# Feed-forward by seven products of halves, in a layer on one core

## The chip, the core and the metric

The program runs on one of the eight cores of a Trainium2 chip. A core has TensorE (PE in the profile, with its weight loads as PEld), VectorE (DVE), ScalarE (ACT), GpSimd (POOL) and SyncE (SP), which here issues the transfers. Operands lie in SBUF, 128 partitions wide; TensorE writes to PSUM, eight banks of 512 float32 columns for each partition. The metric is the device time of the whole program in microseconds, as the median of several runs.

## The reference

One layer of a decoder with two streams: a prompt of 1024 tokens and a sample of 64, side by side as N = 1088 tokens. After two kinds of attention and an attention over a memory comes the feed-forward, to which the change belongs. The model is 1024 wide, the features within are 2816. All is float32.

```python
def mem_attend(h, mk, mv, w_mq, g_mq, w_mo):
    b, t, _ = h.shape
    q = rms_norm((h @ w_mq).reshape(b, t, H_M, HEAD_DIM_M), g_mq)
    return attend(q, mk, mv, None, None).reshape(b, t, D_MODEL) @ w_mo

def conv_ffn(h, prev, w_up, w_conv, b_conv, w_down):
    gu = h @ w_up
    gate, val = gu[..., :D_FF], gu[..., D_FF:]
    t = gate.shape[1]
    gp = jnp.concatenate([prev.astype(gate.dtype), gate], axis=1)
    conv = sum(gp[:, j:j + t] * w_conv[j] for j in range(CONV_W)) + b_conv
    y = (jax.nn.silu(conv) * val) @ w_down
    return y, gp[:, -(CONV_W - 1):]
...
        xp = xp + mem_attend(rms_norm(xp, g_norm2[l]), mk, mv, w_mq[l], g_mq[l], w_mo[l])
        f, conv_p = conv_ffn(rms_norm(xp, g_norm3[l]), zeros_prev, w_up[l], w_conv[l], b_conv[l], w_down[l])
        xp = xp + f
```

## The kernel before

**Precision.** Every matrix product is done as three. Each operand is split into a high part in a reduced float32 form (fp32r) and a low part, the rest. ACT casts the high part, and POOL or DVE subtracts it for the low one. `SPLIT` (three pairs) then multiplies high by high, high by low and low by high into the same PSUM bank.

**Order.** The program is written as one list of instructions, from which the build makes a queue for each engine, and the semaphores between them. Within a queue, instructions run in the order that the build fixed. `place` puts extra steps behind certain pieces of a product. SyncE's queue holds the transfers.

**Activations** lie transposed: eight blocks of 128 rows of the model's width, with the 1088 tokens along the columns. `CHUNKS` cuts these into 384, 384 and 320. A `Product` (872) is one block of 128 outputs for one chunk: `gemm` (859) goes through eight blocks of rows with three matmuls each, 24 in all.

**Weights** come through `Stream` (831). It fetches halves of a block of columns (128 x 512, 256 KB, line 840), three on their way, and splits four ahead: ACT casts (848), POOL subtracts (849). The list `srcs` holds the order: `w_o`, `w_mq`, `w_mo`, then `w_up`.

**Memory output projection.** `project` (984) takes `oT`, the memory attention's output in two parts, through `w_mo` in 8 x 3 products; beside the first of them lies the rest of the attention. For each product DVE adds the residual (1001), SyncE stores the sum to DRAM (1002), ACT and DVE make the two parts of the next operand times the norm's gain (1004, 1005), ACT squares and POOL sums the squares (1011). `after_mo` (1191) makes the root mean squares of a chunk with a matmul of ones (1194), whose result multiplies the up projection's outputs, later.

**Feed-forward.** 22 tiles of 128 features run one after the other (`Tile`, 1235). `run` goes through the gate's three chunks: DVE multiplies each by the norm into a padded row (1269). Then comes the convolution: an ACT pass (1272), two DVE passes over 1090 columns (1274), Silu on ACT (1276), the norm again on POOL (1280). The value's three chunks follow: DVE multiplies (1287), ACT and POOL split the result (1288, 1289). Between their pieces lies the down projection of the tile before (`down`, 1292): for 8 blocks of outputs and 3 chunks three matmuls each (1298), whose results DVE adds to `y` in SBUF (1305). `split_down` splits the tile's down weights on ACT and POOL (1255, 1256).

Of the kernel before, what the change touches and what calls it, by code (L numbers as in the profile page):

```python
# [33 lines left out]
CHUNKS = ((0, 384), (384, 384), (768, 320))  # L34


@with_exitstack
def hybrid_step(ctx: ExitStack, tc: tile.TileContext, i: dict, o: dict):
# [3 lines left out]
    def f32(ap):  # L42
        return ap.bitcast(F32)
# [48 lines left out]
    ps = ctx.enter_context(tc.tile_pool(name="ps", bufs=1, space=PSUM))  # L92
# [58 lines left out]
    def load_x(c, z):  # L151
        """Half of the columns of 256 tokens, or of the sample's 64."""
# [45 lines left out]
    # K, V and Q of a pair of heads over 256 tokens  # L198
# [14 lines left out]
    def qk_norm(p, sq, raw, eps_ap, rows):  # L213
        """q and k of raw [rows, 256], each head's normed, twice in a row; k with its gain, for the cache."""
# [16 lines left out]
    def gained(hi, lo, src, g, rows=slice(0, P)):  # L231
        """The two parts of src with the gain of its rows; the second of some rows alone."""
# [17 lines left out]
    def place(main, subs):  # L250
        """main, and after some of its parts others."""
# [6 lines left out]
    def proj(p, t, subs):  # L258
        """One block of tokens through a pair's columns, woven with subs; what is to be done with it later."""
# [79 lines left out]
    def forget():  # L339
        """log sigmoid of the forget logits, and their running sums."""  # L340
# [4 lines left out]
        # z = exp(-|f|); log1p(z) = log(u) - ((u - 1) - z) / u with u = 1 + z  # L345
# [44 lines left out]
    def toeplitz(head, q, n):  # L390
        """Row r of q reads the head's reversed table from 128 - r on."""
# [20 lines left out]
    class Attn:  # L412
        """Two blocks of 128 queries of one head."""
# [106 lines left out]
    def substeps(slow=False):  # L520
        """What runs between a projection's products: scores of the next head, values of the one before."""
# [54 lines left out]
    # ------------------------------------------------------------------ memory keys and values, sample's attention  # L576
# [70 lines left out]
    class Sample:  # L647
        """The sample's 64 queries of both heads of a pair, one above the other."""
# [94 lines left out]
        def turn(self, c):  # L743
            """Weights of four blocks of 128 keys, or of the new ones, turned."""
# [79 lines left out]
    late_left = ExitStack()  # L824
    stream = None

    # ------------------------------------------------------------------ products with streamed weights
    srcs = [i[n][m][:, 4 * c:4 * c + 4] for n, nm in (("w_o", 8), ("w_mq", 8), ("w_mo", 8)) for m in range(nm) for c in range(2)]
    srcs += [i["w_up"][m][:, 4 * c:4 * c + 4] for f in range(NF) for m in (f, NF + f) for c in range(2)]

    class Stream:
        """Halves of 128 columns of weights in the order of their use, four of them split, three on their way."""
# [10 lines left out]
        def upto(self, n):  # L843
            while self.n < min(n, len(srcs)):
# [4 lines left out]
                pool.tensor_tensor(lo, raw, f32(hi), op=ALU.subtract)  # L849
# [4 lines left out]
        def done(self, j):  # L854
            """Half j isn't used any more."""
# [3 lines left out]
    def gemm(out, j, x, c, end):  # L859
        """The products of halves j and j + 1 with a chunk of tokens, in eight pieces."""  # L860
        c0, cn = CHUNKS[c]

# [9 lines left out]
    class Product:  # L872
        """A chunk of 128 outputs' products, its tile taken at the first."""

        def __init__(self, j, x, c, end, tag="pj"):
            self.tag, self.t = tag, None
            self.pieces = gemm(self.out, j, x, c, end)
# [9 lines left out]
    def parts(pl, name):  # L887
        """Two parts of eight rows of all tokens."""
        return [[pl.tile([P, N + 4], F32R, name=f"{name}{x}{k}")[:, :N] for k in range(KT)] for x in range(2)]

    def open_left():
        nonlocal stream
        left.close()
        ha = late_left.enter_context(tc.tile_pool(name="ha", bufs=1, side="left"))
        stream = Stream(late_left.enter_context(tc.tile_pool(name="wr", bufs=1, side="left")))
        x = late_left.enter_context(tc.tile_pool(name="x0", bufs=1, side="left")).tile([P, 384], F32, name="x0")
        nc.sync.dma_start(x, i["xT"][0, :, 0:384])
        stage = rest.enter_context(tc.tile_pool(name="stage", bufs=1, side="left"))
# [57 lines left out]
    # ------------------------------------------------------------------ output projection  # L956
# [7 lines left out]
    def wide():  # L964
        return [[t[:, k] for k in range(KT)] for t in (hb.tile([P, KT, N], F32R, name=x) for x in ("hhi", "hlo"))]

    BUFS = {"qhi": 2, "qlo": 2, "kvraw": 2, "s": 3}

    def tmp(tag, shape):
        return pl.tile(shape, F32R, name=tag, bufs=BUFS.get(tag, 1))  # L970

    def row(tag, n=384):
        """A row of float32 in a slot of this tag."""
        shape = [P, 2, 384] if tag in ("qhi", "qlo") else [P, 2, 256]
# [9 lines left out]
    def project(j, x, order, firsts, res, out, nxt, gi, accs, after):  # L984
        """res + x @ w, to DRAM; its two parts times the next norm's gain; its squares' sums."""
# [33 lines left out]
    h2 = wide()  # L1019
# [13 lines left out]
    # ------------------------------------------------------------------ memory attention  # L1033
# [3 lines left out]
    oT = parts(ha, "a")  # L1037
# [18 lines left out]
    class Mem:  # L1056
        """A head's attention of a chunk of tokens."""
# [7 lines left out]
        def query(self):  # L1065
            """The products, and what follows each half of them."""
# [72 lines left out]
        def value(self, d):  # L1139
# [28 lines left out]
    for n, u in enumerate(mems):  # L1168
# [4 lines left out]
        def move(h, what):  # L1173
            """Splits this and loads the one after the next."""
# [13 lines left out]
    h3 = wide()  # L1188
    norms = {}

    def after_mo(c, acc):
        cn = CHUNKS[c][1]
        st = bank("PT")[:, :cn]
        pe.matmul(st, ones, acc[:, :cn], start=True, stop=True)  # L1194
        ms, y, a = row("qlo", 768), row("qlo", 768), None
        ms, y, a = ms[:, 0:cn], ms[:, 384:384 + cn], y[:, 0:cn]
        dve.tensor_scalar(ms, st, EPS, None, op0=ALU.add)
        act.activation(y, ms, ACT.Ln)
        act.activation(y, y, ACT.Exp, scale=-0.5)
        dve.tensor_tensor(a, ms, y, op=ALU.mult)  # L1200
# [221 lines left out]
```

## Time and profile before

| | us |
|---|---|
| median of 3 runs | 1882.5 |
| runs | 1881.01 to 1883.11 |
| span of the profiled execution | 1878.9 |
| its end of TensorE's work | 1874.8 |

The span goes from the first to the last instruction of one profiled execution; the runs' time is that of the whole program. The page's second part shows the span in 40 slices, busy tenths of each engine, and the clock that TensorE was granted:

```profile
PE   6899999999997899999999999999999999999999
DVE  6777766767766875334443345445545545555546
ACT  5656666767766665335543332212212212222220
POOL 5646666877976443434433444434434434443441
PEclk9999999999998999999999999999999999999999
```

A slice is 47 us, and the feed-forward takes the last 17 of them. The parts shown below use the same columns as the page: a group's line, engine, operation, output and inputs, shapes and count, then its busy time and the mean of one in ns, then the idle time of its engine before it and what ended that. In the timeline the first number is the start, the second the length.

### The profile page before, as it was taken

The page shows a single profiled execution, that of the slowest core. Times are in us where ns is not written, and L with a number is a line of the kernel's source. Part 1 is how long each engine was busy: PE and PEld are TensorE (multiplying, and loading weights), DVE is VectorE, ACT ScalarE, POOL GpSimd, SP SyncE. Part 2 cuts the span into 40 slices and gives each one's busy share as a digit, 9 for nine tenths or more (in the row PEclk, how much of TensorE's full clock was granted, in tenths as well). Part 3 has the DMA queues.
Part 4 walks back from the last instruction along what each step waited for, and adds up shares of the span by engine and source line. Part 5 has one row for each costly group of instructions (what it writes and reads, how often), then busy time and mean ns, then how long its engine had stood idle before and what let it go on. Part 6 is the DMA issues. An engine that isn't in the chain of part 4 may idle for free.

```text
span 1878.9 us, 31543 instructions
## 1 busy us (share of the span) xinstructions
PE 1808.8 (96%) x11426; PEld 1754.7 (93%) x11426; DVE 1071.5 (57%) x2537; ACT 800.9 (43%) x1828; POOL 937.4 (50%) x1312
## 2 busy tenths in 40 slices
PE   6899999999997899999999999999999999999999
PEld 5789999999996788999999999999999999999999
DVE  6777766767766875334443345445545545555546
ACT  5656666767766665335543332212212212222220
POOL 5646666877976443434433444434434434443441
PEclk9999999999998999999999999999999999999999
DMA  8312122212216776421113433111111111111102
GB/s 276 89 45 68 43 76 77 63 55 76 60 34 177 248 227 196 144 67 52 60 52 122 137 104 106 45 40 51 40 45 51 35 51 45 40 51 40 45 23 97
DMA packets 111339, 157.49 MB, mean 84 GB/s; under 512 B 15480, under 2 KB 75000, under 8 KB 111184
## 3 DMA queue, kind: packets, MB, share of 16 engines
q1 hardware_dynamic: 111184, 155.48, 26.6%
q8 instruction: 90, 1.47, 0.3%
q14 instruction: 65, 0.53, 0.1%
HBM read 125.40 MB, written 33.18 MB: 84 GB/s over the span
## 4 chain that ended last, share of the span: by engine, by line
PE 54%; POOL 1%; issue 1%; ACT 0%; DVE 0%; POOLq 0%; DVEq 0%; ACTq 0%
PE pj L866 37%; PE PT L1298 7%; PE tq L1298 3%; PE O L1298 3%; PE S L1110 1%; PE O L1146 1%; PE tq L1146 1%; POOL lo L849 1%; PE PT L1133 0%; PE O L1110 0%; PE PT L1091 0%; POOL s L1125 0%; PE PT L1194 0%; ACT hi L848 0%; PE PT L1026 0%
## 5 line engine op out<-in xcount | busy, mean ns | idle before, releaser
L866 PE MATMUL pj<-hhi,hi 128*128 128x384 f32 (+1 forms) x1248 | 412.8, 331 | 0.0
L866 PE MATMUL pj<-hlo,hi 128*128 128x384 f32 (+1 forms) x1248 | 408.8, 328 | 0.0
L866 PE MATMUL pj<-hhi,lo 128*128 128x384 f32 (+1 forms) x1248 | 408.3, 327 | 0.0
L849 POOL TENSOR_TENSOR lo<-raw,hi 128x512 fp32r<-128x512 f32 x136 | 176.9, 1302 | 336.7 <-ACT hi L848 336.0
L848 ACT CAST hi<-raw 128x512 fp32r<-128x512 f32 x136 | 84.1, 620 | 406.5 <-issue 253.0
L866 PEld LDWEIGHTS pj<-hhi,hi 128*128 128x128 f32 x1248 | 234.5, 188 | 0.5
L866 PEld LDWEIGHTS pj<-hlo,hi 128*128 128x128 f32 x1248 | 234.6, 188 | 0.1
L866 PEld LDWEIGHTS pj<-hhi,lo 128*128 128x128 f32 x1248 | 234.4, 188 | 0.1
L1305 DVE TENSOR_TENSOR a<-PT,a 128x384 f32<-128x384 f32 (+1 forms) x252 | 133.9, 531 | 158.2 <-PE PT L1298 158.2
L268 PE MATMUL pj<-whi,xhi 128*128 128x384 f32 (+1 forms) x512 | 195.5, 382 | 7.9 <-ACT xhi L126 6.7
L866 PE MATMUL pj<-a,hi 128*128 128x384 f32 (+1 forms) x736 | 183.5, 331 | 3.6 <-DVE qhi L1001 1.7
L268 PE MATMUL pj<-whi,xlo 128*128 128x384 f32 (+1 forms) x512 | 175.7, 343 | 5.9 <-DVE xlo L127 5.9
L268 PE MATMUL pj<-wlo,xhi 128*128 128x384 f32 (+1 forms) x512 | 177.2, 346 | 2.9 <-POOL wlo L119 2.9
L866 PEld LDWEIGHTS pj<-a,hi 128*128 128x128 f32 x736 | 129.4, 188 | 6.2 <-DVE a L909 2.5
L454 ACT ACTIVATE s<-s,mx 128x640 f32<-128x640 f32 (+7 forms) x128 | 94.2, 736 | 79.1 <-DVE mx L452 77.5
L491 DVE TENSOR_TENSOR ptl<-PT,pth 128x512 fp32r<-128x512 f32 (+2 forms) x192 | 99.6, 522 | 38.8 <-ACT pth L490 36.5
L866 PE MATMUL pj<-a,lo 128*128 128x384 f32 (+1 forms) x368 | 120.7, 329 | 0.0
L220 POOL TENSOR_TENSOR r<-m,mhalf 128x4 f32<-128x4 f32 (+1 forms) x72 | 73.8, 1025 | 90.0 <-DVE m L219 80.0
L268 PEld LDWEIGHTS pj<-whi,xhi 128*128 128x128 f32 x512 | 100.0, 196 | 8.9 <-ACT xhi L126 6.7
L268 PEld LDWEIGHTS pj<-whi,xlo 128*128 128x128 f32 x512 | 98.0, 191 | 6.6 <-DVE xlo L127 6.6
L268 PEld LDWEIGHTS pj<-wlo,xhi 128*128 128x128 f32 x512 | 99.6, 195 | 4.5 <-POOL wlo L119 4.5
L490 ACT CAST pth<-PT 128x512 fp32r<-128x512 f32 (+2 forms) x192 | 85.1, 449 | 38.2 <-PE PT L489 36.8
(443 smaller groups left out, 4465.2 us busy)
## 6 DMA issues: line engine op xcount, KB each, us to landing
raw<-in_w_up_dram SPq DMA_DIRECT2D x88, 256.0 KB, 2.6
kvraw<-in_w_down_dram SPq DMA_DIRECT2D x44, 256.0 KB, 2.5
wraw<-in_w_dram SPq DMA_DIRECT2D x56, 192.0 KB, 2.4
mwraw<-in_w_mkv_dram SPq DMA_DIRECT2D x16, 512.0 KB, 5.6
s<-in_xn_dram SPq DMA_DIRECT2D x8, 512.0 KB, 6.8
mixd<-mix SPq DMA_DIRECT2D x32, 128.0 KB, 1.8
bias<-negc SPq DMA_DIRECT2D x8, 512.0 KB, 3.6
raw<-in_w_o_dram SPq DMA_DIRECT2D x16, 256.0 KB, 3.5
```

What stands on the lines that cost most here:

```text
L220: pool.tensor_tensor(r[:rows], m[:rows], mhalf[:rows, 0:4], op=ALU.pow)
L268: pe.matmul(pj[:, :nw], x2[a][:, k, t * P:(t + 1) * P], wt[k][b][:, :nw], start=n == 0, stop=n == 3 * KT - 1)
L454: act.activation(s[:, :n], s[:, :n], ACT.Exp, bias=mx, scale=-1.0, accum_out=sm)
L490: act.copy(hi[:, f:f + n, j], pt[:, f:f + n])
L491: dve.tensor_tensor(lo[:, f:f + n, j], pt[:, f:f + n], f32(hi[:, f:f + n, j]), op=ALU.subtract)
L848: act.copy(hi, raw)
L849: pool.tensor_tensor(lo, raw, f32(hi), op=ALU.subtract)
L866: pe.matmul(out()[:, :cn], w[a][:, k % 4], x[b][k][:, c0:c0 + cn], start=k == 0 and n == 0, stop=k == KT - 1 and n == 2)
L1110: pe.matmul(sp[:rows], self.q[a][:, d, t * P:t * P + rows], k[b][:, d], start=n == 0, stop=n == 5)
L1146: pe.matmul(op[:, a0:a1], v[x][:, b, d * P:(d + 1) * P], self.p2[y][:, b, a0:a1], start=n == 0, stop=n == 5)
L1298: pe.matmul(d[:, :cn], self.wd[x][m // 4][:, (m % 4) * P:(m % 4 + 1) * P], self.a[w][:, c0:c0 + cn], start=z == 0, stop=z == 2)
L1305: dve.tensor_tensor(dst, d[:, :cn], dst, op=ALU.add)
```

## The change

Two matrices cut in halves both ways can be multiplied with seven products of halves in place of eight, if sums of the halves are formed before and after. The change does this with the feed-forward's two projections. For each, A is the weights and B the activations; H = 544 is half of the tokens and Q = 272 half of that.

- **The products.** M1 = A11 B11, M2 = A12 B21, M5, M6, M7, M3 and M4 use sums. Up, an output tile is two blocks of 128 features that are 11 blocks apart (`n` even: two gate blocks, odd: the two value blocks of the same features). Each product is 4 blocks of rows x 3 split pairs x 2 quarters of 272 columns, 24 matmuls.
- **Sums of results in PSUM.** M6, M7 and M4 go on top of M1 in one tile of two banks (chain X), M3 on top of M5 (Z), M2 alone (T). ACT copies M1, M5 and M6 out to SBUF before the next one lands on top; DVE reads the four results.
- **Sums of weights** and all splits of the feed-forward are made by DVE, with ACT's cast; `prepare` runs five products ahead, with seven places for split operands and seven for raw quarters.
- **Sums of activations** (right sums) for the up projection are made during the memory output projection, which now runs for the first half of the tokens and then, with `w_mo` fetched and split again, for the second half. The low parts of the second round's weights are DVE's.
- **Between the projections** the products of gate and value go to DRAM (`ad`), and come back as B's quarters.
- **Down**, one product runs through all 11 steps of features for four output blocks at a time, in four PSUM tiles, before the next product begins; the last two steps run together, block by block. The order is M2, M1, M5, M3, M6, M7, M4. `prepare_down` runs two steps ahead, with three places for the right operand and five for the left. The residual's rows are loaded into `y` before; at the end of M1 ACT copies its result out, and over the steps that follow POOL adds the copy to two other quarters and the residual to a third.

The core of the diff:

```diff
-srcs = [i[n][m][:, 4 * c:4 * c + 4] for n, nm in (("w_o", 8), ("w_mq", 8), ("w_mo", 8)) for m in range(nm) for c in range(2)]
-srcs += [i["w_up"][m][:, 4 * c:4 * c + 4] for f in range(NF) for m in (f, NF + f) for c in range(2)]
+srcs = [i[n][m][:, 4 * c:4 * c + 4] for n, ms in (("w_o", range(8)), ("w_mq", range(8)), ("w_mo", ROWS), ("w_mo", ROWS)) for m in ms for c in range(2)]
...
-                pool.tensor_tensor(lo, raw, f32(hi), op=ALU.subtract)
+                (dve if self.n >= 48 else pool).tensor_tensor(lo, raw, f32(hi), op=ALU.subtract)
...
+CHAIN = {"M1": "X", "M6": "X", "M7": "X", "M4": "X", "M2": "T", "M5": "Z", "M3": "Z"}
+order = [(n, x) for n in range(NF) for x in ("M1", "M2", "M6", "M5", "M7", "M3", "M4")]
...
+def prepare(g):
...
+    if what == "M6":
+        dve.tensor_tensor(a21, a21, a22, op=ALU.add)
+        dve.tensor_tensor(a11, a21, a11, op=ALU.subtract)
+    if what == "M7":
+        dve.tensor_tensor(a21, a22, a11, op=ALU.subtract)
+    if what == "M3":
+        dve.tensor_tensor(a12, a12, a11, op=ALU.subtract)
+    two_parts(hi, lo, src)
...
+def t_sums(m, x):
+    j = m % 4
+    if m < 4:
+        dve.scalar_tensor_tensor(t, x, g3[m], told[j], op0=ALU.mult, op1=ALU.subtract)
+        two_parts(*quarter_of("12", j), t)
+    else:
+        t = t12[j]
+        dve.scalar_tensor_tensor(t, x, g3[m], t, op0=ALU.mult, op1=ALU.subtract)
+        two_parts(*tsum["M6"][j], t)
+        gained_parts(m, *quarter_of("22", j), x)
+        dve.tensor_tensor(told[j], t, told[j], op=ALU.subtract)
+        dve.tensor_tensor(told[4 + j], told[4 + j], t, op=ALU.subtract)
...
+def finish(n, what, w):
+    if what in ("M1", "M5", "M6"):
+        kept[n, what] = temps.take()
+        act.copy(halves(kept[n, what]), both(w))
+        return
+    r, z, other = {"M2": (0, 0, "M1"), "M7": (1, 1, "M5"), "M3": (0, 1, "M6"), "M4": (1, 0, None)}[what]
+    if is_gate:
+        gate.into(r, z, w, t)
+    elif t is None:
+        value(gate, r, z, w, None)
+    else:
+        add(t, w, t)
+        value(gate, r, z, None, t)
...
+for g, (n, what) in enumerate(order):
+    w = product(n, what, lambda p, j: hi_lo[p][:, j * P:(j + 1) * P], 4, [right(what, j) for j in range(4)], True, True)
+    if g == 0:
+        t3_parts()
+        norm3(1)
+        t4_parts()
+    finish(n, what, w)
+    while prepared < min(len(order), g + 1 + AHEAD):
+        prepare(prepared)
+        prepared += 1
...
+def prepare_down(s):
...
+    if what == "M5":
+        dve.tensor_tensor(S, S, a["A22"], op=ALU.add)
+        dve.tensor_tensor(b12, b12, b11, op=ALU.subtract)
+    if what == "M3":
+        dve.tensor_tensor(S, S, a["A11"], op=ALU.subtract)
+        dve.tensor_tensor(a["A12"], a["A12"], S, op=ALU.subtract)
...
+    two_parts(*la, left)
+    two_parts(*ra, right)
...
+for s, (what, f) in enumerate(steps):
+    if f < NG - 1:
+        prepare_down(s + 2)
+        load_a()
...
+            load_b(DOWN[nxt], f)
...
+    for m in range(4):
+        for x in ((s,) if f < NG - 2 else (s, s + 1)):
+            la, ra = down_ops[x]
+            for z in range(2):
+                for y, (p, b) in enumerate(SPLIT):
+                    pe.matmul(ws[m][:, z, :Q], la[p][:, m * P:(m + 1) * P], ra[b][:, z * Q:z * Q + Q],
+                              start=first and y == 0 and what in opening, stop=final and y == 2 and what in closing, skip_group_check=True)
+        if f == NG - 2:
+            finish_down(what, m, ws[m])
```

`Gate.into` adds a result and the kept copy into the padded row on DVE (in three pieces for the second half of the tokens), and starts `conv` for a block once both halves are in: DVE multiplies by the norm, ACT's pass, two DVE passes of 1090, Silu on ACT, and DVE multiplies by the norm again. `two_parts` is ACT's cast and DVE's subtraction. `value` multiplies with the gate on DVE and stores to `ad`. `finish_down` adds a block's result in PSUM to its rows of `y` on DVE.

More of the change, by code (lines that the diff above doesn't have):

```diff
@@ L1018, in hybrid_step @@
     dve.memset(e2, 1.0)
-    h2 = wide()
+    h2 = [[t[:, k] for k in range(KT)] for t in (hq.tile([P, KT, N], F32R, name=x) for x in ("hhi", "hlo"))]
     def after_o(c, acc):
@@ L1186, in hybrid_step @@
         place(u.query(), subs)
[L1188 to L1198, printed above, removed]
+    queries.close()
+    hr = ctx.enter_context(tc.tile_pool(name="hr", bufs=1, side="right", reuse_waits="tile"))
@@ new lines, in hybrid_step, with wide_rows, halves, both @@
+    PLACES = ("11", "21", "12", "22")
+    def wide_rows(b, p, dt=F32R):
+        return hr.tile([P, 4, H], dt, name=f"h{b}{p}")
+    h3 = {b: [wide_rows(b, p) for p in range(2)] for b in PLACES[:2]}
+    accs, rs = [None, None], [None, None]
+    g3 = [gcol[:, 2, m:m + 1] for m in range(KT)]
+    def halves(ap):
+        return ap.rearrange("p (z q) -> p z q", z=2)
+    def both(w):
+        return w[:, :, :Q]
+    def like(ap, src):
+        return ap if len(src.shape) == 2 else halves(ap)
+    def long_row(tag):
+        return row(tag, 768)[:, :H]
@@ L1199, in after_mo, with norm3 @@
+    def norm3(z):
+        w = wides.take()
+        for q in range(2):
+            pe.matmul(w[:, q, :Q], ones, accs[z][:, q * Q:q * Q + Q], start=True, stop=True)
+        a, y = (long_row("qlo") for _ in range(2))
+        rs[z] = long_row(("ptl", "sq")[z])
+        dve.tensor_scalar(halves(a), both(w), EPS, None, op0=ALU.add)
+        act.activation(y, a, ACT.Ln)
         act.activation(y, y, ACT.Exp, scale=-0.5)
-        dve.tensor_tensor(a, ms, y, op=ALU.mult)
+        dve.tensor_tensor(a, a, y, op=ALU.mult)
@@ L1212, in hybrid_step @@
-    for n, g in enumerate(project(32, oT, ORDER, [], x1d, xd, h3, 2, ("kPh", "kPl", "kSh"), after_mo)):
-        subs = [(at - 8 * n, f) for at, f in last if 0 <= at - 8 * n < 8] + take()
-        if n == 2:
-            subs += [(0, lambda: mems[-1].value(0)), (1, lambda: mems[-1].value(1))]
-        place(g.pieces, subs)
-    rows_ = [ha.tile([P, N + 4], F32R, name=f"a{x}{k}") for x in range(2) for k in range(KT)]
-    y = [f32(r) for r in rows_[:8]]
-    acts = [[rows_[8 + 2 * b + z][:, :N] for z in range(2)] for b in range(2)]
@@ new lines, in hybrid_step, with right, product @@
+    tsum = {}
+    def right(what, j):
+        if what in ("M1", "M2", "M3", "M5"):
+            return quarter_of({"M1": "11", "M2": "21", "M5": "12", "M3": "22"}[what], j)
+        return tsum[what][j]
+    chains = {}
+    def product(key, what, a, k, rights, begin, end):
+        chain = key, CHAIN[what]
+        if chain not in chains:
+            chains[chain] = wides.take()
+        w = chains[chain]
+        fresh, final = what in ("M1", "M2", "M5"), what in ("M4", "M2", "M3")
+        for z in range(2):
+            for j in range(k):
+                for x, (p, b) in enumerate(SPLIT):
+                    pe.matmul(w[:, z, :Q], a(p, j), rights[j][b][:, z * Q:z * Q + Q],
+                              start=fresh and begin and j == 0 and x == 0, stop=final and end and j == k - 1 and x == 2, skip_group_check=True)
+        return w
@@ new lines, in hybrid_step @@
+    for w_, m in enumerate(ROWS):
+        nc.sync.dma_start(told[m], xd[m, :, 0:H])
+        act.mul(told[m], told[m], g3[m])
+    for n, m in enumerate(ROWS):
+        x = long_row("qhi")
+        nc.sync.dma_start(x, x1d[m, :, H:N])
+        w = wides.take()
+        for q in range(2):
+            place(gemm(lambda: w[:, q], 48 + 2 * n, oT[1], (q * Q, Q), q == 1), [])
+            if n == 0 and q == 0:
+                norm3(0)
+        evict_mo(m, 1, 0, H, both(w), x)
+        wides.give(w)
+        t_sums(m, x)
@@ new lines, in hybrid_step @@
+    sums = [row("qlo", 768)[:, :512], row("qlo", 768)[:, :512]] + [row(x, 768)[:, :512] for x in ("pth", "ptl", "sq")]
+    sums += [f32(flat(x)) for x in ("vSh", "vSl", "vPh", "vPl", "kSh", "kSl")]
+    raws = Slots([lambda: f32(flat("kvraw"))] * 2 + [lambda: stream_place("raw")] * 3)
+    parts_ = Slots([lambda: (stream_place("hi"), stream_place("lo"))] * 4 + [lambda: (flat("kPh"), flat("kPl"))])
+    NEEDS = {"M2": ("A12",), "M1": ("A11",), "M5": ("A21", "A22"), "M3": ("A11", "A12"), "M6": (), "M7": ("A22",), "M4": ("A22",)}
@@ new lines, in hybrid_step, with load_a @@
+    loads = [(s, a) for s, (what, f) in enumerate(steps) for a in NEEDS[what]]
+    downs = {}
+    def load_a():
+        while loads:
+            s, a = loads[0]
+            f = steps[s][1]
+            if a == "A21":
+                t = sums[f]
+            elif raws.free:
+                t = raws.take()
+            else:
+                break
+            loads.pop(0)
+            downs[s, a] = t
+            r, c = int(a[1]) - 1, int(a[2]) - 1
+            nc.sync.dma_start(t, i["w_down"][f + c * NG, :, r * 512:r * 512 + 512])
```

371 lines of the change are left out of this document (276 added, 95 removed).

## The prediction

> **What bounds the kernel now.** I read the page first, then the busy time by stretch, cut where the lines change.
>
> ```profile
> span 1878.9 us, 31543 instructions
> PE 1808.8 (96%) x11426; PEld 1754.7 (93%) x11426; DVE 1071.5 (57%) x2537; ACT 800.9 (43%) x1828; POOL 937.4 (50%) x1312
> 0.00:977.60 977.60, 914.15 (x6026) 862.76 (x6027) 619.19 (x1707) 595.57 (x1502) 576.00 (x900) 0.98 0.34 104
> 977.60:1082.30 104.70, 104.49 (x643) 103.46 (x642) 38.75 (x73) 39.58 (x82) 43.49 (x43) 1.00 0.40 124
> 1094.30:1876.00 781.70, 780.47 (x4711) 779.91 (x4709) 408.12 (x749) 159.95 (x235) 309.58 (x362) 1.00 0.17 52
> ```
>
> The stretches are PE, PEld, DVE, ACT, POOL, then granted clock, DMA share, GB/s. Up to 977.6 the code stays; from there to 1082.3 runs the memory output projection, then the feed-forward. There TensorE is busy 780.47 of 781.70 us at clock 1.00, VectorE about half. Only TensorE's work counts, so the first question is what one matmul costs at the new width of 272 columns (before: 384, 384, 320). A matmul's recorded length overlaps its neighbours; the pitch of starts is the cost.
>
> ```profile
> 1400.14 0.34 PE L866 MATMUL pj<-hhi,hi 128*128 128x384 f32 x1
> 1402.05 0.34 PE L866 MATMUL pj<-hhi,lo 128*128 128x384 f32 x1
> 1409.42 0.31 PE L866 MATMUL pj<-hhi,hi 128*128 128x320 f32 x1
> 1411.03 0.31 PE L866 MATMUL pj<-hhi,lo 128*128 128x320 f32 x1
> 911.78 0.28 PE L1110 MATMUL S<-kPh,qhi 128*128 128x256 f32 x1
> 912.38 0.28 PE L1110 MATMUL S<-kPh,qlo 128*128 128x256 f32 x1
> 908.83 0.28 PE L1146 MATMUL O<-pth,vSl 128*128 128x64 f32 x1
> 909.16 0.28 PE L1146 MATMUL O<-pth,vSl 128*128 128x64 f32 x1
> ```
>
> First and last of an unbroken row: 11 steps of 384 columns in 1.91 us are 0.1736 each; 11 of 320 in 1.61, 0.1464; 5 of 256 in 0.60, 0.120; 3 of 64 in 0.33, 0.11. The first three lie on a line; the last shows the floor of a weight load. At 272 the line gives 0.120 + 16/64 x 0.0264 = 0.1266, above the floor. Its hard ends are the neighbours, 0.120 and 0.1464; I take 0.1266, sixteen columns from the nearer row.
>
> **TensorE's work.** Before, the projection is 8 x 24 x (2 x 0.1736 + 0.1464) = 94.8 us. After, it runs two halves of tokens in two quarters: 8 x 2 x 2 x 24 = 768 matmuls, 97.2 us. Before, the feed-forward is 4752 matmuls: 3168 x 0.1736 + 1584 x 0.1464 = 781.9 us, and the 781.70 us stretch with 4711 of them says that this is nearly all of its time. After: 22 tiles x 7 products x 4 blocks x 3 x 2 = 3696 going up, 7 x 11 steps x 24 = 1848 going down, 5544 in all, 701.9 us. So +2.4 - 80.0 = **-77.6 us**. One product or step is 24 x 0.1266 = 3.04 us: the clock for all that follows.
>
> The Trainium skill, "TensorE: Matmul & The Clock Gate", section "Wait — 56ns, not 53.3ns?", puts a warm matmul at its columns over 2.4 GHz and 2.5 ns. By that, an estimate, 5328 matmuls before take 818 us and 6312 after take 731, a gain of 87 us; the row of 320 columns (0.1464 against the page's 0.136) disagrees, and the row decides.
>
> **Is VectorE the next bound?** It takes over POOL's splits and gains, and all new sums.
>
> ```profile
> L491 DVE TENSOR_TENSOR ptl<-PT,pth 128x512 fp32r<-128x512 f32 x72 | 49.4, 690 | 19.0 <-ACT pth L490 18.9
> L909 DVE TENSOR_TENSOR a<-mraw,a 128x1024 fp32r<-128x1024 f32 x8 | 9.8, 1241 | 1.5 <-ACT a L908 1.3
> L1269 DVE TENSOR_TENSOR a<-pj,ptl 128x256 f32<-128x256 f32 x22 | 9.4, 425 | 27.2 <-PE pj L866 27.2
> L1269 DVE TENSOR_TENSOR a<-pj,ptl 128x64 f32<-128x64 f32 x22 | 4.7, 215 | 0.0
> L1274 DVE SCALAR_TENSOR_TENSOR a<-a,sq,a 128x1090 f32<-128x1090 f32 x44 | 77.4, 1758 | 11.1 <-ACT a L1272 10.3
> L601 DVE TENSOR_TENSOR mwlo<-mwraw,mwhi 128x512 fp32r<-128x512 f32 x16 | 17.9, 1121 | 2.3 <-ACT mwhi L600 2.2
> ```
>
> Between these I read 0.69 us for 512 elements, 0.72 for 544, 0.66 for 480, 0.44 and 0.37 for 272 and 208, 0.215 for 64. L601 (1.121 for 512, both inputs in SBUF, POOL working) shows such work near double beside POOL. Going up POOL has only small copies left, so I use the short figures and 1.31 for 1090 (1.241 plus 66 elements), with 1.76 as the other end.
>
> Per tile, weights need 7 low parts and 4 sums: 11 x 0.69 = 7.6. A gate tile adds its four PSUM passes, 0.72 + 1.03 + 1.03 + 0.72 = 3.5, and two convolutions, 5.8 + 5.1 (gains 1.6 or 0.9, two passes 2.62, gains 1.6). A value tile adds 5.4. A pair: 15.2 + 14.4 + 5.4 = **35.0 of 42.5 us** of TensorE. A step going down needs 0.69 + 0.72 and up to two sums, at most 2.8 of 3.04. VectorE fits, without much room. At 1.76 a pair is 36.8, and still fits.
>
> The weight casts are ACT's as before:
>
> ```profile
> L848 ACT CAST hi<-raw 128x512 fp32r<-128x512 f32 x136 | 84.1, 620 | 406.5 <-issue 253.0
> L1272 ACT ACTIVATE a<-a,sq 128x1090 f32<-128x1090 f32 x22 | 28.7, 1304 | 18.5 <-DVE a L1269 16.8
> L1276 ACT ACTIVATE a<-a 128x1090 f32<-128x1090 f32 x22 | 24.6, 1119 | 69.7 <-DVE a L1274 69.7
> ```
>
> A pair costs ACT 14 casts (8.7), 6 copies of 544 (about 4) and 4.8 of convolution, 17.5 of 42.5.
>
> **The new waits.** One PSUM accumulator (chain X) holds M1, then M6, M7, M4 on top, and between them is read: ACT copies M1 and M6, VectorE adds M7. The next product of the chain must wait, but each time another product of 3.04 us stands between, and the copy takes about 0.7. So it costs only when the reading engine is over 2.3 us late. What is queued before it matters, and that order is not the program's:
>
> ```profile
> 1402.23 0.46 PE L1298 MATMUL PT<-a,kPh 128*128 128x320 f32 x2
> 1402.43 0.56 DVE L1269 TENSOR_TENSOR a<-pj,pth 128x384 f32<-128x384 f32 x1 [1.53 <-PE pj L866]
> 1402.90 0.48 DVE L1305 TENSOR_TENSOR a<-PT,a 128x320 f32<-128x320 f32 x1
> 1084.53 0.91 PE L1194 MATMUL PT<-kPl,ones 128*128 128x384 f32 x2 [1.23 <-POOL kPl L1011]
> 1090.89 0.81 PE L1194 MATMUL PT<-kSh,ones 128*128 128x320 f32 x2 [1.11 <-POOL kSh L1011]
> ```
>
> The code writes the sums at 1305 ahead of 1269, and VectorE ran 1269 first: the build fixes each queue by when it reckons things ready. Where it reckons wrong, TensorE stands, 1.23 and 1.11 us here. In the tightest stretch, from a gate's M3 to the value's M7, VectorE has 6.8 + 5.8 + 1.4 + 8 x 0.69 = 19.6 us for six products, 18.2. It is 1.4 us behind when M7 must be read, within the slack. I charge 0.7 us a pair, 8 us.
>
> **Starts and ends.** Attention's tail lies beside shorter products: 1.5 us (0 to 4). Two norms take the place of three; the waits that go (1.23, 1.11, about 0.2) are replaced: 0 (-2.5 to 3). At the first tile, M1 and M2 use sums ready long before, but M6 needs a load into a buffer that the last right sum holds: 4 us of VectorE (0.72 x 5 and a hand-off), a load, two sums, a split, 0.69 x 3.
>
> ```profile
> raw<-in_w_up_dram SPq DMA_DIRECT2D x88, 256.0 KB, 2.6
> 0.00:47.00 47.00, 30.91 (x145) 28.12 (x146) 28.22 (x89) 25.89 (x67) 25.73 (x45) 0.96 0.85 276
> 610.00:660.00 50.00, 43.96 (x293) 37.88 (x293) 44.38 (x115) 32.87 (x87) 24.65 (x24) 0.97 0.77 249
> 560.00:610.00 50.00, 37.15 (x249) 33.73 (x247) 32.53 (x70) 35.11 (x75) 32.05 (x44) 0.86 0.57 168
> ```
>
> 4 + 2.6 + 2.1 = 8.7, and hand-offs, against 6.1 of M1 and M2: I charge 4 (0 to 15, if all loads come late). From up to down, the first operands use slots freed three products earlier: 3 (0 to 15, if eleven 278 KB loads go ahead of the first weights at 276 GB/s). Each of the seven down products ends in four PSUM adds with the third operand slot just released: 0.7 each, 5 (0 to 20). The w_mo weights fetched and split twice hide: 1.4 us of VectorE in 6.1 a row.
>
> The same page's "Part 1: The HAM clock gate" halves the clock after an idle window of about 3.4 us; the 0.86 beside PE 37.15 of 50 bears it out. By it two starts of 4 us would cost about 3.4 more; the sum leaves it out.
>
> Losses: 8 + 1.5 + 4 + 3 + 5 = 21.5. **-77.6 + 21.5 = -56.1**, a span of 1822.8. The median of the runs stands 3.6 above the span (1882.5 against 1878.9): **1826**.
>
> **Rivals.**
> 1. *Slower: VectorE and ACT hold the convolution in the order written.* VectorE then stands through both ACT passes (1.30 + 1.12 and 0.2), and ACT's copy of the next M1 waits behind the second Silu, some 16.7 us after M3's end (6.84 + 2.6 + 5.5 + 1.1 + 0.7), where M6 wants X after three products, 9.1: 7.6 a pair, 84 us in place of 8. 1826 + 76 = 1902; slower from 5.8 a pair on ((77.6 - 13.5)/11). For it: 1.23 us of misjudgement above. Against: the reordered rows. 0.10.
> 2. *The chain in PSUM binds in part*: 3 a pair, 33 in place of 8: 1851. The 2.3 us slack is thin against one ACT pass of 1.30 and one of 1.12 in the way. 0.15. The Trainium skill, "PSUM — Partial Sum Buffer", section "PSUM bank collisions raise a hardware error", says that no two engines may touch a bank at once, so the wait can't be relaxed.
> 3. *Loads bind going down.* M5 needs 262 + 262 + 278 KB per step, 264 GB/s; M2 with its residual rows 9.3 MB in 33 us, 280. The best rows are 276 and 249. At 231 to 249 both stages lose about 11: 1837. 0.15.
> 4. *No loss at all*, or the change doing exactly what its count says: 1805. 0.12.
>
> My forecast has 0.48. The range 1803 to 1866 takes in 2, 3 and 4 and the greater part of the losses' ends; the pitch of 0.120 would lie below (-42 more), that of 0.1464 above (+125), both excluded for most of their length by the straight line. About 0.2% (3.8 us) is what a measurement here can tell from no change: faster 0.87, same 0.02, slower 0.11.
>
> **What would show it.** The 272-wide pitch at 0.1266 (0.125 to 0.128); PE stretches going up with 42.5 us a pair and little idle; waits of TensorE for X: below 1 us a pair, else rival 1 or 2 (a Silu in the chain says 1); idle TensorE behind DMA in M2 or M5 says 3; POOL near empty and VectorE's 1090 pass at about 1.3 us. I am wrong if VectorE's SBUF sums stay near 1.1 us without POOL: a pair would be over 42.5 and VectorE the bound.

## The result, and the profile after

| | before | after |
|---|---|---|
| median of 4 runs, us | 1882.8 | 1811.67 |
| runs | 1881.01 to 1883.11 | 1811.5 to 1812.76 |
| span of the profiled execution | 1878.9 | 1809.8 |

The runs before are the three shown above and one more. The ratio is 0.9625, its interval 0.9611 to 0.9639. The span is 69.1 us shorter; 56.1 were forecast. First the page of the changed kernel:

```profile
span 1809.8 us, 34045 instructions
...
PE 1724.4 (95%) x12412; PEld 1668.5 (92%) x12412; DVE 1226.5 (68%) x2693; ACT 929.6 (51%) x2042; POOL 683.9 (38%) x1042
...
PE   6899999999997898999999999999999999998999
...
DVE  5777667677676788333444378877777777677974
```

VectorE rises from about half to seven and eight tenths, and TensorE's row stays at nine; in the fourth slice from the end it drops for a moment. The stretches, with the columns of the prediction's:

```profile
983.50:1091.60 108.10, 107.01 (x840) 105.89 (x839) 59.90 (x101) 54.55 (x103) 41.73 (x42) 1.00 0.58 177
1106.00:1562.30 456.30, 456.30 (x3640) 456.30 (x3638) 349.41 (x596) 182.18 (x265) 41.38 (x84) 1.00 0.27 88
1562.30:1622.90 60.60, 60.60 (x488) 60.60 (x487) 39.95 (x62) 23.37 (x41) 0.00 (x0) 1.00 0.93 317
1622.90:1644.00 21.10, 13.73 (x82) 12.93 (x81) 20.18 (x23) 6.28 (x11) 14.69 (x10) 0.84 0.71 225
1644.00:1806.00 162.00, 161.04 (x1284) 160.38 (x1283) 118.50 (x181) 58.33 (x100) 5.49 (x6) 1.00 0.26 85
```

After the first tile TensorE doesn't stand once going up (456.30 of 456.30), nor in M2, where the transfers move 317 GB/s. What is lost going down lies mostly in the 21 us behind M1: 13.73 busy, at a clock of 0.84.

**The pitch**, read as in the prediction. In the timeline of the changed kernel these two rows are 84 matmuls apart (28 times three), 10.52 us, so 0.1252 each; the line had given 0.1266.

```profile
1299.84 0.41 PE L1381 MATMUL W<-h,hi 128*128 128x272 f32 x2
...
1310.36 0.41 PE L1381 MATMUL W<-h,kPh 128*128 128x272 f32 x2
```

**The ledger.** Stages are cut at the first matmul of each in the timelines (before: 977.65 and 1082.79; after: 983.58 and 1091.62), and end with the last one (1874.84 and 1805.88):

| us | before | after | difference |
|---|---|---|---|
| up to the memory output projection | 977.65 | 983.58 | +5.9 |
| that projection | 105.1 | 108.0 | +2.9 |
| feed-forward | 792.05 | 714.3 | -77.8 |
| tail | 4.1 | 3.9 | -0.1 |

The feed-forward's 5544 matmuls are 694.1 us at 0.1252. The 20.2 above that are 8.0 at the first tile (470.7 going up against 3696 x 0.1252 = 462.7) and 12.2 going down (243.6 against 231.4). TensorE's waits in it, with total, times and longest:

```profile
PE W L1678 <- DVE gp L1452: 5.5, 2, 3.7
PE W L1678 <- DVE f L1246: 2.2, 2, 1.8
PE W L1381 <- ACT f L1245: 1.0, 1, 1.0
PE W L1381 <- ACT kSh L1245: 0.8, 1, 0.8
PE W L1381 <- DVE gp L1452: 0.8, 1, 0.8
PE W L1381 <- DVE kSl L1246: 0.7, 1, 0.7
PE W L1381 <- ACT hi L1245: 0.7, 1, 0.7
```

The first two are, but for 0.36 us later on, the hand-over from M1 to M5 going down, where results in PSUM must be read (1452) and splits made (1246); the five others, 4.0 us in all, are the first tile.

Four questions were left for experiments: what makes the front 5.9 us later, whether TensorE or VectorE sets the up stage, what "sums on DVE alone" is worth, and what stalls M1 to M5 and the first tile.

### The profile page after: what moved, and what is told of

Same layout as the page of the kernel before. It is cut to its first block, busy times and chain, and to the rows that moved or that the text cites. A ratio compares the mean times of both kernels' runs of the same rounds, so it can differ in the third digit from the quotient of the medians.

```text
span 1809.8 us, 34045 instructions
## 1 busy us (share of the span) xinstructions
PE 1724.4 (95%) x12412; PEld 1668.5 (92%) x12412; DVE 1226.5 (68%) x2693; ACT 929.6 (51%) x2042; POOL 683.9 (38%) x1042
## 4 chain that ended last, share of the span: by engine, by line
PE 47%; DVE 4%; issue 1%; DMA 1%; POOL 1%; ACT 1%; SPq 0%; POOLq 0%; DVEq 0%; ACTq 0%
PE W L1381 25%; PE W L1678 9%; PE pj L869 7%; PE W L869 2%; PE S L1124 1%; PE tq L1160 1%; PE O L1160 1%; POOL lo L852 1%; DVE lo L1246 1%; DMA kvraw<-in_w_down_dram 0%; PE PT L1147 0%; DMA raw<-in_w_down_dram 0%; DVE f L1246 0%; PE O L1124 0%; DMA f<-x2d 0%
## 5 line engine op out<-in xcount | busy, mean ns | idle before, releaser
L1678 PE MATMUL W<-f,hi 128*128 128x272 f32 x672 | 129.2, 289 | 7.7 <-DVE gp L1452 5.5
L1381 PE MATMUL W<-h,hi 128*128 128x272 f32 x704 | 134.2, 288 | 0.7 <-ACT hi L1245 0.7
L1678 PEld LDWEIGHTS W<-f,hi 128*128 128x128 f32 x672 | 106.4, 190 | 8.8 <-DVE gp L1452 6.0
L1381 PEld LDWEIGHTS W<-h,hi 128*128 128x128 f32 x704 | 110.7, 188 | 0.9 <-ACT hi L1245 0.9
L1381 PE MATMUL W<-h,lo 128*128 128x272 f32 x352 | 101.8, 289 | 0.0
L1678 PE MATMUL W<-f,lo 128*128 128x272 f32 x336 | 97.4, 290 | 0.0
L227 POOL TENSOR_SCALAR qk<-qkraw,r 128x128 f32<-128x128 f32 x256 | 92.7, 379 | 6.0
L493 PE MATMUL PT<-ident,s 128*128 128x128 f32 x528 | 90.2, 276 | 4.9 <-DVE ptl L495 3.8
L869 PE MATMUL pj<-a,hi 128*128 128x384 f32 (+1 forms) x352 | 89.5, 337 | 0.4 <-DVE qhi L1005 0.4
L453 PE MATMUL S<-kh,q 128*128 128x256 f32 (+1 forms) x304 | 76.8, 278 | 12.0 <-DVE mx L456 10.2
```

Source lines behind the costliest of these rows:

```text
L227: pool.tensor_scalar(qk[:rows, h], raw[:rows, h * 64:(h + 1) * 64].rearrange("p (o d) -> p o d", o=1).broadcast_to([rows, 2, 64]), r[:rows ...
L453: pe.matmul(sp[:, a:a + (k1 - k0) * P], q, kk[:, h, src], start=m == 0, stop=m == 1)
L493: pe.transpose(pt[:, b - ch[0]], self.s[j][:, (b - w0) * P:(b - w0 + 1) * P], ident)
L869: pe.matmul(out()[:, :cn], w[a][:, k % 4], x[b][k][:, c0:c0 + cn], start=k == 0 and n == 0, stop=k == KT - 1 and n == 2)
L1381: pe.matmul(w[:, z, :Q], a(p, j), rights[j][b][:, z * Q:z * Q + Q], start=fresh and begin and j == 0 and x == 0, stop=final and end and j ...
L1678: pe.matmul(ws[m][:, z, :Q], la[p][:, m * P:(m + 1) * P], ra[b][:, z * Q:z * Q + Q], start=first and y == 0 and what in opening, stop=fina ...
```

## The experiments

Ratios are against the kernel before, run on the same chip, whose median was 1881.4 to 1881.9. Differences in us from the change are against its median of 1811.67, measured beside a median before of 1882.8; so about 1 us of each can come from the chip.

### The front: the order of the pools

The code up to the projection is the same, but its first rows differ. Stalls of TensorE in the changed kernel's timeline around 712:

```profile
713.83 0.42 PE L782 MATMUL PT<-ident,su 128*64 128x128 f32 x1 [3.36 <-DVE su L778]
717.34 0.69 PE L869 MATMUL pj<-a,lo 128*128 128x384 f32 x1 [1.39 <-POOL lo L852]
```

The change opens one pool of SBUF (`ha`) after the stream's pools and first loads instead of ahead of them. `e1_pools` does that alone, in the kernel before:

```diff
-        ha = late_left.enter_context(tc.tile_pool(name="ha", bufs=1, side="left"))
         stream = Stream(
...
         nc.sync.dma_start(x, i["xT"][0, :, 0:384])
+        ha = late_left.enter_context(tc.tile_pool(name="ha", bufs=1, side="left"))
```

> The kernel before, with one part of the change alone: the buffers of the streamed weights and of the first residual are placed under those of the mix, where the change has them, and no longer above. Theory: this alone is why the output projection began 5.9 us later after the change (TensorE stood 3.4 and 2.0 us there); then this kernel takes 4 to 7 us more than before, 1887 to 1890. Rival: the delay comes from something else in the changed program; then it takes as long as before, within 1.5 us.

1888.17 (1882.06 to 1890.48), ratio 1.0036 [1.0022, 1.005]: some 7 us, 4 to 9 by the interval, with the same two stalls in its timeline:

```profile
712.59 0.30 PE L778 MATMUL PT<-ident,su 128*64 128x128 f32 x1 [2.76 <-DVE su L774]
713.84 1.01 PE L866 MATMUL pj<-a,hi 128*128 128x384 f32 x2 [0.30 <-ACT hi L848]
716.11 0.69 PE L866 MATMUL pj<-a,lo 128*128 128x384 f32 x1 [1.27 <-POOL lo L849]
```

So the order of the pools makes the front later. How much is read from the runs, since single executions scatter: among the traces of the changed kernel and its variants up to `e10_both` the feed-forward starts between 1089.6 and 1095.8. The transfers show how. These are the first loads of the output projection's weights, in the kernel before and in the changed one, and what the change's transfer ahead of them (899) waited for:

```profile
583.00 1.38 SPq L840 DMA_DIRECT2D raw<-in_w_o_dram  x3
```

```profile
708.47 1.37 SPq L843 DMA_DIRECT2D raw<-in_w_o_dram  x3
```

```profile
SPq L899 <- DMA vmd<-kv: 1.4, 1, 1.4
```

The first loads go out 125 us later, once the memory's last store out of `kv` has landed, so TensorE has no products of the projection to fill its waits with at 712. `e1_pools` shows the same wait, of 1.4. `e11_three`, below, moved two other tiles of the memory; there this wait and the 3.36 us stayed. No run moves `kv` itself.

### TensorE's count and pitch

`e2_narrow` gives the kernel before the new width: its feed-forward in four chunks of 272 columns, 6336 matmuls in place of 4752.

```diff
-            for c in range(3):
-                g = Product(48 + 4 * f, h3, c, c == 2)
+            for c in range(4):
+                g = Product(48 + 4 * f, h3, FCH[c], c == 3)
...
+    FCH = tuple((x, 272) for x in range(0, N, 272))
```

> The kernel before with the eight products of halves as they were, but the feed-forward's tokens cut in four chunks of 272 in place of 384, 384 and 320: 6336 matmuls at 272 columns where there were 4752. It prices the narrower matmul alone. Theory: at the pitch of 0.1252 that the changed kernel's trace shows, 793.3 us for 781.9, so +11 us, 1894. At the forecast pitch of 0.1266 it would be +20, 1903. Rival: the changed program's lower pitch is due to its other order of operands and not to the width; then +20 or more. A time at or below that of before would say that the width itself brought part of the gain.

1902.38 (1898.93 to 1902.88), 1.0114 [1.0101, 1.0127], +21. Two windows of it; in the later one 800 matmuls fill 100 us, 0.125 each:

```profile
1100.00:1200.00 100.00, 94.83 (x739) 92.82 (x738) 45.57 (x107) 23.21 (x35) 39.96 (x52) 1.00 0.29 87
...
1400.00:1500.00 100.00, 100.00 (x800) 100.00 (x799) 50.86 (x128) 19.32 (x32) 38.64 (x48) 1.00 0.13 40
```

The pitch is a matter of the width alone, then, with no part of the new scheme in it. At the prediction's pitches it explains 10 of the 21 (6336 x 0.125 = 792.0 against 781.9), and only 4 at the mean pitch that the old kernel really had (787.6 for its 4752 matmuls, from the long window; see the section on the prediction). In the profiled execution the feed-forward is 14.8 us longer (806.8 against 792.05); some 5 of them lie at the start, where TensorE is busy 94.83 of 100 us. Another 3.3 come ahead of it, in code that is the same, and 4.0 behind its last matmul. What makes these was not followed.

`e3_twice` computes M2 twice, 528 more matmuls with no new load, sum or split:

```diff
-        w = product(n, what, lambda p, j: hi_lo[p][:, j * P:(j + 1) * P], 4, [right(what, j) for j in range(4)], True, True)
+        for _ in range(2 if what == "M2" else 1):
+            w = product(n, what, lambda p, j: hi_lo[p][:, j * P:(j + 1) * P], 4, [right(what, j) for j in range(4)], True, True)
```

> The changed kernel with the product M2 of each of the 22 tiles going up computed twice, the second overwriting the first in the same bank: 528 matmuls more on TensorE and nothing on another engine. Theory, TensorE sets the time going up: 528 x 0.1252 = +66 us, 1878. Rival, VectorE already sets it: the extra work fills TensorE's waits and costs less than 20 us.

1875.65 (1873.47 to 1878.09), 0.9969 [0.9956, 0.9981]: 64.0 more than the change, for a count of 528 x 0.1252 = 66.1. TensorE sets the up stage.

### VectorE: how much room, and in which order

`e5_dve_once` and `e6_dve_twice` repeat each subtraction of a weight's low part going up once and twice (154 and 308 more passes, 105 and 210 us by their mean of 0.683):

```diff
         two_parts(hi, lo, src)
+        for _ in range(1):
+            dve.tensor_tensor(lo, src, f32(hi), op=ALU.subtract)
```

> The changed kernel with each low part of the weights going up subtracted twice over by VectorE, to the same place: 154 passes of 512 more, 0.69 us each by the trace, 106 us in all, or 97 at the pitch of passes that follow each other. VectorE was busy 349 of 456 us there, so it would be just full. Theory, VectorE is hidden until it is full: +0 to +10 us, 1812 to 1822. Rival, VectorE is already on the path: the greater part of the 106 us shows, over +50.

1815.68 (1811.41 to 1817.94), 0.9652 [0.9636, 0.9668], span 1809.3: hidden, or nearly. VectorE had 106.9 us free of 456.30.

> As the run before, with two passes more for each low part, 212 us, or 194 at the pitch. VectorE would need 543 to 561 us where TensorE needs 456. Theory: VectorE becomes the bound and the stage takes its time: +85 to +110 us, 1897 to 1922. Were the time unchanged by it, the trace's account of VectorE would be wrong.

1880.16 (1875.14 to 1882.69), 0.9986 [0.9975, 0.9997], +68: with that, VectorE is the bound. Its window and its waits, from the trace of `e6_dve_twice`:

```profile
1400.00:1500.00 100.00, 90.09 (x709) 88.78 (x708) 99.02 (x172) 35.00 (x52) 15.17 (x16) 1.00 0.21 69
```

```profile
PE W L1383 <- DVE lo L1358: 38.3, 17, 4.5
```

It is less than the 85 to 110 expected, and the timeline says why: the seventh of an unbroken row of passes, each 0.68 long, begins 3.62 us after the first.

```profile
1403.55 0.68 DVE L1358 TENSOR_TENSOR lo<-kvraw,hi 128x512 fp32r<-128x512 f32 x1
...
1407.17 0.68 DVE L1358 TENSOR_TENSOR kPl<-raw,kPh 128x512 fp32r<-128x512 f32 x1
```

So a pass back to back costs 0.603, not its length; VectorE's rows overlap like TensorE's. At 0.603 the 308 passes are 186 us, 79 above the room: near the 68.

`e4_in_order` is rival 1: VectorE's and ScalarE's queues going up (between the two `BOUNDS`) keep the order in which the code is written, in place of the build's.

```diff
-            if out is not None and f"{engine} {out.tensor.name.rpartition('_')[0]}" in ORDERED:
+            if out is not None and (f"{engine} {out.tensor.name.rpartition('_')[0]}" in ORDERED
+                                    or BOUNDS[0] <= at < BOUNDS[1] and engine in ("Activation", "DVE")):
...
```

> The changed kernel with the instructions of VectorE and ScalarE going up held in the order in which the program writes them, the rest as it was. This is rival 1 of the prediction made true. Theory on record: VectorE stands through both ACT passes of each convolution and the copy of the next M1 waits behind the second Silu, 7.6 us a pair of tiles, 84 us: 1895. If only a part of it binds, 3 us a pair: 1845. Rival: the order is of no weight, since the operands are made five products ahead: within 8 us of 1812.

1946.8 (1943.56 to 1950.14), 1.0354 [1.0339, 1.0369], +135. Its waits from 1110 to 1560, and a window:

```profile
PE W L1381 <- ACT qlo L1517: 34.5, 5, 6.9
PE W L1381 <- ACT qhi L1517: 20.8, 3, 6.9
PE W L1381 <- DVE lo L1246: 7.1, 8, 0.9
```

```profile
1500.00:1600.00 100.00, 82.96 (x614) 81.54 (x613) 59.81 (x96) 31.43 (x47) 2.11 (x14) 0.91 0.20 65
```

The wait is the one that the rival described, for ACT's copy of a result behind the convolution (1517), and near its size, 6.9 a time against 7.6. Over the whole stage these waits are 88.2 us in 12, close to the 84 on record, so the price was short in what comes on top. Shorter waits, for splits and copies, are 17.0; and TensorE also runs slower (clock 0.91 in the window, where 614 matmuls are busy for 82.96 us, against 76.9 at 0.1252). The order of the two queues was worth some 135 us, nearly twice what the change gained, and it is the build that makes it.

`e7_pool_lows` gives the subtractions going up back to POOL.

```diff
-        two_parts(hi, lo, src)
+        two_parts(hi, lo, src, pool)
```

> The changed kernel with the low parts of the weights going up made by POOL and no longer by VectorE, as the kernel before made them. POOL then has 154 x 1.3 = 200 us of the 456, VectorE loses 106 us of work, but its passes over two operands in SBUF get longer beside POOL. Theory, both stay below TensorE's time: the time stays within 5 us of 1812. Rival, what POOL does to VectorE makes VectorE late for the accumulators: +20 us or more.

1834.42 (1833.0 to 1835.77), 0.9747 [0.9733, 0.9762], +22.7: the rival was right and "within 5" wrong. VectorE's rows from 1110 to 1550, first of the change, then of `e7_pool_lows`:

```profile
L1491 DVE SCALAR_TENSOR_TENSOR t<-gp,s,t 128x1090 f32<-128x1090 f32 x44 | 58.4, 1347 | 0.0
```

```profile
L1491 DVE SCALAR_TENSOR_TENSOR t<-gp,s,t 128x1090 f32<-128x1090 f32 x40 | 63.2, 1600 | 1.5
L1486 DVE TENSOR_TENSOR gp<-gp,sq 128x480 f32<-128x480 f32 x20 | 30.0, 1498 | 0.0
```

```profile
1110.00:1550.00 440.00, 418.60 (x3288) 416.03 (x3287) 325.48 (x403) 163.03 (x241) 226.48 (x221) 0.99 0.23 75
```

VectorE was relieved of some 100 us of work and yet stays busy for 325 of 440 us (336.65 in the change): beside a working POOL its passes within SBUF take longer, 480 elements 1.50 in place of the 0.66 that the prediction had. TensorE then waits for ACT, whose copies (1517) come behind the slowed convolution; the longest of its waits in the same window:

```profile
PE W L1381 <- ACT f L1517: 16.8, 9, 1.9
```

### The first tile, and M1 to M5

Going down, this is VectorE (and one POOL row) of the change where TensorE stands:

```profile
1626.50 0.69 DVE L1603 TENSOR_TENSOR kSh<-kSh,kvraw 128x512 f32<-128x512 f32 x1 [0.89 <-DMA kvraw<-in_w_down_dram]
1627.23 1.75 DVE L1607 TENSOR_TENSOR raw<-raw,qlo 128x512 f32<-128x512 f32 x1
1628.91 1.86 DVE L1246 TENSOR_TENSOR kPl<-pth,kPh 128x512 fp32r<-128x512 f32 x1
...
1633.44 0.71 DVE L1452 TENSOR_TENSOR gp<-W,gp 128x544 f32<-128x544 f32 x1
```

```profile
1628.38 1.84 POOL L1633 TENSOR_TENSOR f<-f,t 128x544 f32<-128x544 f32 x1
```

Passes of 512 go from 0.69 to 1.75 and 1.86 while POOL adds M1's copies (1632, 1633), and the PSUM read that M5 needs comes late: TensorE's waits of 3.72 and 1.81 end with such reads. The wait of 1.84 that ends at 1625.07 is not POOL's, whose first add starts at 1626.68. `e8_later_sums` moves POOL's sums to the steps of M6 and M7:

```diff
...
-        if later:
+        if later and what in ("M6", "M7"):
             later.pop(0)()
```

> The changed kernel with POOL's sums of M1's result, and of the residual, put off from the steps of M5 to those of M6 and M7. Theory: around the change from M1 to M5 TensorE lost about 9 us since VectorE's passes took 1.3 to 1.9 us beside POOL in place of 0.69; then the time falls by 5 to 9 us, to 1803 to 1807. Rival: the loads of M5 are the cause (the transfers were busy 0.94 of the time just before, and VectorE waited for landings); then it falls by less than 3.

1814.69 (1812.0 to 1816.19), 0.9645 [0.9631, 0.9658]: not faster, against expectation; by the time alone the rival, M5's loads, would hold. But the gaps behind M1 shrink (from 7.4 to 3.6 us in the timelines), and new ones open in M6, where VectorE is full (first window below): the slow passes go where POOL goes.

The first tile: M6's first load goes to a buffer that the last right sum holds, as the prediction saw. `e9_raw_order` lets the stream's three places, free by then, take those first quarters.

```diff
-    raws = Slots([lambda: f32(flat("kvraw"))] * 2 + [lambda x=x: f32(flat(x)) for x in ("vSh", "vSl")] + [lambda: stream_place("raw")] * 3)
+    raws = Slots([lambda: f32(flat("kvraw"))] * 2 + [lambda: stream_place("raw")] * 3 + [lambda x=x: f32(flat(x)) for x in ("vSh", "vSl")])
```

> The changed kernel with the first quarters of the up weights loaded to the buffers of the stream first, and last to the two that the right sums still hold. Theory: TensorE's 8 us at the first tile come from M6's weights, loaded into a held buffer; then the time falls by 3 to 6 us, to 1806 to 1809. Rival: VectorE's own queue of right sums is what M6 waits for; then it falls by less than 1.5.

1808.03 (1805.15 to 1811.55), 0.9615 [0.9599, 0.9632]. The two intervals of the ratio, this one and the change's, overlap, so the stage decides: going up takes 466.6 us in place of 470.7. The five waits are gone; one behind the norm has come:

```profile
PE W L1292 <- POOL pth L1242: 2.7, 1, 2.7
```

`e10_both` has both edits.

> Both of the last two edits together. Theory: they add up, 8 to 15 us, 1797 to 1804. Rival, neither cause is right: within 3 us of the changed kernel.

1813.02 (1811.74 to 1813.96), 0.9637 [0.9624, 0.965]: they don't add up.

`e11_three` keeps both and gives the later sums to VectorE; memory's two wide tiles also go to the top of the stack.

```diff
-    mem = [mp.tile([P, KT, 256], F32R, name=f"m{n}") for n in ("hi", "lo")]
+    mm = left.enter_context(tc.tile_pool(name="mm", bufs=1, side="left"))
+    mem = [mm.tile([P, KT, 256], F32R, name=f"m{n}") for n in ("hi", "lo")]
...
-            later.extend([lambda: pool.tensor_tensor(y_of(m, 1), y_of(m, 1), p, op=ALU.add),
...
+            later.extend([lambda: dve.tensor_tensor(y_of(m, 1), y_of(m, 1), p, op=ALU.add),
...
```

> The changed kernel with three edits: the order of the raw places as in the run on it; the sums put off to M6 and M7 as before, but made by VectorE and no longer by POOL; and the memory's two wide tiles moved from the bottom of their stack, where the streamed weights now land, to its top. Theory: the first brings 4 us as measured; the second removes the slow passes without moving them, 3 to 6; the third lets the first output weights load early, 4 to 6 as the run on the buffers' places showed from the other side. Together 11 to 16, 1796 to 1801. Rival: VectorE has no room for the sums in M6 and the delay at the first output weights has another cause; then only the first edit shows, 1808.

1802.14 (1798.53 to 1806.18), 0.9584 [0.9567, 0.9601]: faster than both kernels, by two of its three edits: the third left the front's wait as it was (above). The same stretch of M6, first with POOL (`e8_later_sums`), then with VectorE alone (`e11_three`):

```profile
1690.00:1740.00 50.00, 44.39 (x339) 42.62 (x339) 50.00 (x71) 16.84 (x30) 14.36 (x12) 1.00 0.14 42
```

```profile
1690.00:1740.00 50.00, 49.90 (x399) 49.67 (x399) 49.79 (x84) 18.83 (x33) 0.00 (x0) 1.00 0.24 79
```

VectorE did 84 passes in place of 71 in the same 50 us, POOL's among them, and TensorE's idle time went from 5.6 us to 0.1. One sum shows it, of 544 columns: on POOL (`e8_later_sums`), then on VectorE (`e11_three`).

```profile
L1632 POOL TENSOR_TENSOR f<-f,t 128x544 f32<-128x544 f32 x4 | 6.9, 1726 | 28.6 <-DVE f L1452 28.6
```

```profile
L1633 DVE TENSOR_TENSOR f<-f,t 128x544 f32<-128x544 f32 x4 | 2.9, 726 | 0.0
```

Its down stage takes 236.6 us (1557.89 to the end of its last matmul, 1794.52) against the change's 243.6. `e10_both`, which has the same sums at the same steps but on POOL, needs 245.7 for it; the tiles that `e11_three` moves besides are no longer in use there. One wait is left in it:

```profile
PE W L1681 <- DVE f L1247: 3.2, 1, 3.2
```

VectorE, whose split ends it, had just stood for down weights that landed late:

```profile
1618.46 0.69 DVE L1604 TENSOR_TENSOR sq<-sq,kvraw 128x512 f32<-128x512 f32 x1 [1.48 <-DMA kvraw<-in_w_down_dram]
```

`e12_spread` loads the residual's rows for M5 over M1's steps, on top of `e11_three`, in case that wait came from loads crowded in M2:

```diff
-            if m < 4 or z:
+            if m < 4 and z == 0:
                 nc.sync.dma_start(y_of(m, z), xd[m, :, z * H:z * H + H])
...
+        if second and what == "M1":
+            m = second.pop(0)
+            nc.sync.dma_start(y_of(m, 1), xd[m, :, H:N])
```

> As the run before, and eight of the twelve loads of residual rows, those of the second half of the tokens, are moved from before the first step going down to the steps of M1, one a step. Theory: the wait of about 2 us as M5 begins comes from loads that queue behind those rows (the transfers are busy 0.94 of the time until then); then it goes, 1 to 3 us below the run before. Rival: M5 asks for 264 GB/s itself and waits as before; within 1 us of the run before, or over it.

1803.59 (1800.83 to 1807.57), 0.9588 [0.9572, 0.9603]: no gain, as its rival said. The wait at M1's end stays (2.4), and others come earlier (1.5 and 0.65). M5's own loads, the rival's reason, fit the late landing above; no run tests them alone.

## Why the prediction was right, and where it wasn't

The direction, the cause and the range held: the feed-forward is TensorE's, its count fell, and the time fell by that count to within a few us. 1811.7 is 14.3 below the number, though, and nearer to rival 4's 1805. Rival 4's reason, no loss, is not what happened. Of the 14.3, 13.0 are the span's (-69.1 against -56.1); the rest is the distance of the median from the span, 3.6 before and 1.9 after. Term by term, for the span:

- **"At 272 the line gives ... 0.1266"**: 0.1252. Over 6312 matmuls this is -8.8 us (7.8 in the feed-forward, about 1 in the projection). `e2_narrow` gives the same 0.125 in the old scheme. The page's rule (the Trainium skill, "TensorE: Matmul & The Clock Gate", section "Wait — 56ns, not 53.3ns?") would give an estimate of 0.1158; the measurement stands against it.
- **"the 781.70 us stretch with 4711 of them says that this is nearly all of its time"** was the step that failed most. The feed-forward of the kernel before took 792.05 from its first matmul at 1082.79, and 781.9 were taken: -10.2, in two parts. Up to 1094.30, where the window began, 43 of its matmuls start, worth 7.5 us at 0.1736, in 11.5 us: 4.0 are two norms and the waits for them, which "Two norms take the place of three ... 0" had set equal. The other 4709 are worth 774.4 us at the prediction's two pitches, and took 780.5 (1094.30 to 1874.84) with hardly a gap. So the two rows of twelve had read the old pitch 0.8% too low: 6.1 us.
- **The losses in the feed-forward** were charged at 20 and came to 20.2, but by luck in the sum. Going up 8 were charged for the chain X and none came; M2's start 3, none; the first tile 4, it was 8.0; the down products 5, it was 12.2. About half of the first tile's loss is the load that the prediction named: without it `e9_raw_order` goes up 4.1 us faster. The down loss is nearly all at M1 to M5, and not four adds at each product's end. The greater part, 7.0 of it, goes when VectorE makes POOL's adds (243.6 to 236.6 in `e11_three`; 245.7 in `e10_both`, with the adds moved but still POOL's). The description of the change names these adds; the prediction gave them no price, though it had quoted L601 at 1.121 beside POOL. The other 5.2 are mostly the wait left in `e11_three`.
- **"Up to 977.6 the code stays"**: it does, and yet it ends 5.9 us later, because of the pools' order (`e1_pools`): +5.9. That no line changes doesn't mean that no buffer moves. With this the terms add up: -8.8 - 10.2 + 0.2 + 5.9 = -12.9.
- **VectorE at 35.0 us a pair**: 349.41 of 456.30 is 32.5 of 42.5. The 1090 pass was 1.347 (1.31 taken). It bound neither the change nor, with 105 us more, `e5_dve_once`.
- **Rival 1** is a real mechanism and was rightly not the likeliest. Its cost was 135 rather than 84 (`e4_in_order`), with 88 of it in the waits that it named.
- **Rival 2** did not occur: the waits for W going up are all in the first tile. **Rival 3** did not in M2, which ran at 317 GB/s without one gap, where 276 had been the best row seen; at the start of M5 it may be in what is left (the late landing in `e11_three`). Its 231 GB/s stand in no row, and at 249 its two losses add up to about 6, not 11.

Right after the 3.7 us wait behind M1 the granted clock was 0.50. The Trainium skill, "TensorE: Matmul & The Clock Gate", section "Part 1: The HAM clock gate", puts TensorE at half its clock after an idle window of about 3.4 us; here this trace agrees.

```profile
1634.00:1637.00 3.00, 2.79 (x11) 2.65 (x12) 3.00 (x5) 0.00 (x0) 3.00 (x3) 0.50 0.61 190
```

## What to carry to other kernels

When a stage is bound by one engine, count its instructions times their pitch, and take the old stage from its first instruction to its last, its own losses included, before the new losses are charged. Work given to a second engine isn't free because that engine is idle: here POOL's adds slowed VectorE's more than they relieved it, and one engine doing all was faster. A change of where buffers lie can move a stage whose code stays.

## What was not expected of the hardware

- Beside a working POOL, VectorE's pass of 512 elements within SBUF took 1.75 to 1.86 us where it takes 0.69. Its PSUM read at 1633.44 stayed at 0.71, though POOL was adding from 1632.93 on.
- POOL's copies of two elements, 187 ns in the kernel before (1270), took 719 ns in the changed one at 1487. At 1466 half of the 22 took under 200 ns and the other half over 1150. VectorE was at work in both kernels; what sets the long ones apart isn't shown.
- VectorE's passes overlap: 0.68 long, 0.603 apart back to back (`e6_dve_twice`).
- The clock also fell where no single wait was over 1.0 us: 0.64 at the last of the first tile's five short ones.

```profile
1104.00:1107.00 3.00, 2.24 (x9) 2.03 (x10) 3.00 (x5) 0.00 (x0) 0.00 (x0) 0.64 0.00 0
```
